# The end of a decoder block's kernel: last weight sums halved early, VectorE's order written down, last tile in two column halves

## The chip, the cores and the metric

One core of one Trainium2 chip runs the kernel. The metric is the device time of one execution in microseconds; the time of a kernel is the median of its runs. TensorE (PE) multiplies matrices into PSUM, VectorE (DVE) and ScalarE (ACT) work on rows of 128 partitions, GpSimd (POOL) takes some element-wise work early on, and SyncE (SP) issues the loads and stores. The engines run side by side and wait for each other through semaphores.

## What is computed

One layer of a hybrid decoder block: two attention branches over the same normed input, gated and merged. For 512 tokens of width 1024 it ends in these lines (u, the projections and both attentions stand ahead of them):

```python
y_mla = (o_mla * jax.nn.silu(z_mla)) @ w_br_mla[l]
...
y_fox = (o_fox * jax.nn.silu(z_fox)) @ w_br_fox[l]
mixed = (jax.nn.sigmoid(gate_a) * y_mla + jax.nn.sigmoid(gate_b) * y_fox) @ w_out[l]
h = h + rmsnorm(mixed, post_norm_g[l])
```

rmsnorm divides each token's row by the root of the mean of its squares, and multiplies by a gain per column. Only the last two lines concern the change.

## The kernel before

Nearly all the work is matmuls in a float32 form. Every operand x is split into hi, a rounded copy made by ScalarE, and lo = x - hi, made by VectorE; a product is three matmuls, hi x hi, hi x lo and lo x hi. A weight piece of 128 x 1024 thus costs a load or a sum, one conversion on ScalarE (`wh`, L130), and one subtraction on VectorE (`wl`, L103). `wh` and `wl` come from pools of three buffers each (`wp`), and a conversion waits until TensorE has left the buffer.

The product with `w_out` runs at the end. The contraction of 1024 is cut into two halves, the tokens into two halves of 256, the output columns into two halves of 512 (N0 and N1), and seven half-size products are formed in place of eight, from sums of weight blocks (`tb`, made earlier by VectorE from loaded blocks) and sums of token blocks (`mx`, halved into slices of `uT0`, called `s_[0]` to `s_[3]`, with hi and lo parts `sh` and `sl`). Each product has two pieces c of the contraction and two token tiles r of 128, and `block` (six matmuls of 128 x 512) does one (c, r). X[r], Z[r] and Y[r] are PSUM tiles of 128 x 512 float32. The order on TensorE, which is taken as written, is: X (plain weights, tokens `a1`), Y (plain, `a2`), Z (`summed(0)`, `s_[0]`), X (`summed(2)`, `s_[1]`), Z (plain, `s_[3]`), X (`summed(1)`, `s_[2]`, called w7), X (`summed(3)`, `a2`, called w4). X and Z keep adding onto what stands in them, and `yo` collects results of the four token tiles t = 0 to 3.

An output tile t ends so: ScalarE squares a half row and sums it (`squares_of`, L1120), VectorE scales that sum (`first_sum`, L1123), multiplies the row by the gain (`scaled_g`, L1127), ScalarE takes the root (L1130), VectorE the reciprocal (L1131), and for each column half VectorE multiplies by it and adds the input x (L1133), after which SP stores it (L1135). Tiles 0 and 1 finish during the product before the last and the last; tiles 2 and 3 need the last product, whose X[0] and X[1] hold their columns N0.

In the kernel before, w4's two pieces go through `summed`, as every sum does: conversion and subtraction into the pool's buffers shortly before the product. The second piece is queued behind VectorE's add that reads X[0] (L1165). The order on VectorE and ScalarE is that of a scheduler, which goes by priorities and by what it takes to be ready. The changed instructions are all behind 559 us.

Of the kernel before, what the change touches and what calls it, by code (L numbers as in the profile page):

```python
# [17 lines left out]
ALU = mybir.AluOpType  # L18
# [4 lines left out]
D = 1024  # L23
# [5 lines left out]
EPS = 1e-6  # L29
# [25 lines left out]
def block_kernel(ctx: ExitStack, tc: tile.TileContext, x, meta_tokens, pre_norm_g, w_in, fox_forget_b,  # L55
                 mla_q_norm_g, mla_kv_norm_g, w_uq, w_ukv, w_br_mla, w_br_fox, w_out, post_norm_g,
                 rope_tok, rope_pe, out):
    nc = tc.nc
# [43 lines left out]
    def split_lo(eng, lo, src, hi):  # L102
        return eng.tensor_tensor(out=lo, in0=src, in1=f32(hi), op=ALU.subtract)  # L103
# [159 lines left out]
    with ExitStack() as ph:  # L263
# [33 lines left out]
        for c in range(4):  # L297
            r = pa.tile([128, 2, NSM], F32, tag="wsr", name=f"wsr{c}", bufs=4)
# [145 lines left out]
        pin = tc.keep_in_program_order  # L444
# [74 lines left out]
        with tc.issue_after(lowered[("k", 1, 0), 1]):  # L519
            nc.vector.tensor_tensor_scan(out=fa[:, 0], data0=fa[:, 1], data1=fa[:, 2], initial=0.0, op0=ALU.add,  # L520
                                         op1=ALU.add)
        ch = pal.tile([NH, 2, L], F32R, tag="ch", name="ch")
        with tc.issue_after(halved[("k", 1, 0), 1]):
# [3 lines left out]
                                       op0=ALU.mult, op1=ALU.subtract)  # L527
# [21 lines left out]
    with ExitStack() as att:  # L549
# [451 lines left out]
    with ExitStack() as mg:  # L1001
# [89 lines left out]
        N0, N1 = slice(0, 512), slice(512, D)  # L1091
# [5 lines left out]
        def summed(n, c):  # L1097
            uid[0] += 1
            raw = tb[n][:, 2 * c : 2 * c + 2].rearrange("p k f -> p (k f)")
            return by_k(wsplit((uid[0], raw, [(0, 1024)], 1024))[0], 2)  # L1100

        def block(ps, a, t0, w, c, r, first, last, cs=slice(0, 512)):

            q = 0
            for kk in range(2):
                k = 2 * c + kk
                ts = slice(t0 + 128 * r, t0 + 128 * r + 128)
                for x, b in ((a[0], w[0]), (a[1], w[0]), (a[0], w[1])):
# [10 lines left out]
        def squares_of(src, t, n, w=512):  # L1119
            nc.scalar.activation(jk[:, :w], src, AF.Square, accum_out=ss[:, t, n : n + 1])  # L1120

        def first_sum(t, n):
            nc.vector.tensor_scalar(out=ss[:, t, 2:3], in0=ss[:, t, n : n + 1], scalar1=1.0 / D, scalar2=4.0 * EPS,  # L1123
                                    op0=ALU.mult, op1=ALU.add)

        def scaled_g(t, sl, src=None):
            nc.vector.tensor_tensor(out=yo[:, t, sl], in0=yo[:, t, sl] if src is None else src, in1=gp[:, sl], op=ALU.mult)  # L1127

        def finish_t(t, n, order):
            nc.scalar.activation(ss[:, t, 3:4], ss[:, t, n : n + 1], AF.Sqrt, bias=ss[:, t, 2:3], scale=1.0 / D)  # L1130
            nc.vector.reciprocal(ss[:, t, 3:4], ss[:, t, 3:4])  # L1131
            for sl_ in order:
                nc.vector.scalar_tensor_tensor(out=yo[:, t, sl_], in0=yo[:, t, sl_], scalar=ss[:, t, 3:4],  # L1133
                                               in1=xr[:, t, sl_], op0=ALU.mult, op1=ALU.add)
                nc.sync.dma_start(out2[128 * t : 128 * t + 128, sl_], yo[:, t, sl_])  # L1135

        X, Z = ([op5.tile([128, 512], F32, tag="po", name=f"{n}{r}") for r in range(2)] for n in "xz")
# [1 line left out]
        s_ = list(zip(sh, sl))  # L1139
# [15 lines left out]
        product(Z, s_[3], 0, lambda c: plain(1, 1, c), False, True)  # L1155
        w7 = [summed(1, c) for c in range(2)]
        for r in range(2):
            nc.vector.tensor_tensor(out=yo[:, r, N1], in0=Z[r], in1=yo[:, r, N1], op=ALU.add)
            squares_of(yo[:, r, N1], r, 1)
        w4 = [summed(3, 0)]  # L1160
        for c in range(2):
            for r in range(2):
                block(X, s_[2], 0, w7[c], c, r, False, False)
                if c:
                    read = nc.vector.tensor_tensor(out=yo[:, 2 + r, N1], in0=X[r], in1=yo[:, 2 + r, N1], op=ALU.add)  # L1165
# [59 lines left out]
```

## Time and profile before

| | us |
|---|---|
| median of 3 runs | 599.7 (599.19 to 601.25) |
| the profiled execution's own time | 599.22 |
| its span, first to last instruction | 597.2 |
| busy: TensorE, VectorE, ScalarE | 588.5, 383.0, 343.6 |
| last matmul ends | 591.16 |
| last store issued | 594.14 |

The profile is of one execution. A row gives the start in us from the span's start, the length in us, the engine, the line of the kernel, the operation, what it writes and reads, and how often it is repeated; in brackets stands how long the engine sat idle before it and what released it. Times of matmuls are modelled at their ends. In a group's row, "busy, mean ns" follows the bar.

### The profile page before, as it was taken

Reading aid. Unit: us, or ns where it says so; the run is one execution under the profiler, and the core shown is the slowest. Engines: PE = TensorE matmul, PEld = TensorE weight load, DVE = VectorE, ACT = ScalarE, POOL = GpSimd, SP = SyncE. Lnnn points to the kernel's source line nnn. Section 1 sums busy time; section 2 is a strip of 40 time slices with the busy share of each in tenths; the row PEclk is TensorE's granted clock in tenths of the full one; section 3 lists DMA queues with packets and bytes.
Section 4 is the critical chain, followed back from the end, with each engine's and each line's share of the span. In section 5 each row is a group of like instructions: output and inputs, shape, how many; then the busy total and the mean of one; then the engine's idle time right before and its main releaser. Section 6 shows DMA issues by size and latency. Waiting matters only on the chain.

```text
span 597.2 us, 10753 instructions
## 1 busy us (share of the span) xinstructions
PE 588.5 (99%) x3707; PEld 497.4 (83%) x3707; DVE 383.0 (64%) x1088; ACT 343.6 (58%) x786; POOL 201.0 (34%) x268
## 2 busy tenths in 40 slices
PE   8999999999999999999999999999999999999995
PEld 6889789889889888898898898878888888888884
DVE  6846776775775775757758747854634524367957
ACT  7847775784774775757748747842123423353753
POOL 4316746455458463554544544430000000000000
PEclk9999999999999999999999999999999999999999
DMA  8533799999986998896996887978523332333603
GB/s 293 117 80 98 152 173 252 211 201 230 170 198 117 222 223 215 183 192 161 173 203 164 195 162 154 193 168 295 168 78 99 105 106 72 105 106 104 213 2 140
DMA packets 219838, 96.91 MB, mean 162 GB/s; under 512 B 131552, under 2 KB 209768, under 8 KB 219784
## 3 DMA queue, kind: packets, MB, share of 16 engines
q1 hardware_dynamic: 219784, 96.23, 68.9%
q8 instruction: 29, 0.48, 0.3%
q14 instruction: 25, 0.20, 0.1%
HBM read 61.82 MB, written 3.97 MB: 110 GB/s over the span
## 4 chain that ended last, share of the span: by engine, by line
PE 95%; ACT 2%; DMA 1%; SPq 1%; issue 0%; DVE 0%; POOL 0%; DVEq 0%; ACTq 0%; POOLq 0%
PE z L97 17%; PE pg L97 15%; PE py L97 15%; PE v L97 9%; PE st L97 8%; PE fk L97 8%; PE fq L97 8%; PE ov L97 5%; PE x L97 4%; PE psm L97 2%; PE mq L97 2%; PE mk L97 1%; DMA wsr<-in_w_in_dram 1%; PE ppe L97 1%; PE y L97 1%; ACT uTh L373 0%
## 5 line engine op out<-in xcount | busy, mean ns | idle before, releaser
L103 POOL TENSOR_TENSOR wl<-wraw,wh 128x1024 fp32r<-128x1024 f32 (+2 forms) x62 | 119.7, 1937 | 95.3 <-ACT wh L130 72.3
L130 ACT CAST wh<-wraw 128x1024 fp32r<-128x1024 f32 (+1 forms) x80 | 83.2, 1042 | 115.6 <-PE pg L97 38.5
L799 ACT ACTIVATE sf<-sf,nb 128x272 f32<-128x272 f32 (+3 forms) x128 | 72.5, 567 | 16.7 <-DVE nb L791 15.4
L827 DVE SCALAR_TENSOR_TENSOR pn<-sf,ri,pn 128x128 f16<-128x128 f32 (+3 forms) x128 | 69.2, 579 | 6.9 <-ACT pn L826 6.6
L103 DVE TENSOR_TENSOR wl<-wraw,wh 128x1024 fp32r<-128x1024 f32 x34 | 41.6, 1223 | 42.4 <-ACT wh L130 42.4
L826 ACT ACTIVATE pn<-sf,ri 128x128 f16<-128x128 f32 (+3 forms) x128 | 61.3, 549 | 10.1 <-ACT sf L799 7.4
L97 PE MATMUL z<-uTh,wh 128*128 128x512 f32 x128 | 51.0, 398 | 0.0
L97 PE MATMUL pg<-uTh,wh 128*128 128x512 f32 x128 | 50.3, 393 | 0.0
L97 PE MATMUL z<-uTl,wh 128*128 128x512 f32 x128 | 50.1, 391 | 0.0
L97 PE MATMUL z<-uTh,wl 128*128 128x512 f32 x128 | 50.0, 391 | 0.0
L97 PE MATMUL pg<-uTl,wh 128*128 128x512 f32 x128 | 49.8, 389 | 0.0
L97 PE MATMUL pg<-uTh,wl 128*128 128x512 f32 x128 | 49.8, 389 | 0.0
L97 PE MATMUL py<-gh,wh 128*128 128x512 f32 x128 | 49.8, 389 | 0.0
L97 PE MATMUL py<-gl,wh 128*128 128x512 f32 x128 | 49.8, 389 | 0.0
L97 PE MATMUL py<-gh,wl 128*128 128x512 f32 x128 | 49.8, 389 | 0.0
L97 PE MATMUL st<-hlk,hlq 64*128 64x272 f32 (+3 forms) x480 | 46.0, 309 | 0.0
L97 PEld LDWEIGHTS st<-hlk,hlq 64*128 64x128 f32 x480 | 34.8, 185 | 6.0 <-ACT vh L714 2.8
L695 DVE TENSOR_REDUCE vsc<-v 128x1 f32<-128x272 f32 (+1 forms) x32 | 13.2, 432 | 37.8 <-PE v L97 37.8
L97 PE MATMUL v<-uTh,wl 128*128 128x256 f32 (+1 forms) x128 | 36.5, 285 | 0.0
L97 PE MATMUL fk<-uTl,wh 128*128 128x256 f32 (+1 forms) x128 | 36.4, 285 | 0.0
L97 PE MATMUL fk<-uTh,wh 128*128 128x256 f32 (+1 forms) x128 | 36.4, 285 | 0.0
L97 PE MATMUL v<-uTl,wh 128*128 128x256 f32 (+1 forms) x128 | 36.4, 285 | 0.0
(240 smaller groups left out, 1464.1 us busy)
## 6 DMA issues: line engine op xcount, KB each, us to landing
wraw<-in_w_in_dram SPq DMA_DIRECT2D x56, 512.0 KB, 4.5
wraw<-in_w_br_fox_dram SPq DMA_DIRECT2D x8, 512.0 KB
tb<-in_w_out_dram SPq DMA_DIRECT2D x8, 512.0 KB, 6.7
wraw<-in_w_br_mla_dram SPq DMA_DIRECT2D x8, 512.0 KB, 3.4
cbp<-c_dram SPq DMA_DIRECT2D x14, 264.0 KB, 5.4
wraw<-in_w_out_dram SPq DMA_DIRECT2D x6, 512.0 KB, 6.0
xr<-in_x_dram SPq DMA_DIRECT2D x4, 512.0 KB
out_dram<-yo SPq DMA_DIRECT2D x8, 256.0 KB, 2.0
```

What stands on the lines that cost most here:

```text
L97: nc.tensor.matmul(*a, **k)
L103: return eng.tensor_tensor(out=lo, in0=src, in1=f32(hi), op=ALU.subtract)
L130: nc.scalar.copy(wh[:, :n], raw[:, :n])
L695: nc.vector.tensor_reduce(out=sc[:, i : i + 1], in_=ps, op=ALU.max, axis=AX.X, apply_absolute_value=True)
L799: exps[g] = nc.scalar.activation(sf, sf, AF.Exp, bias=sums["nb"][:, h, b : b + 1], scale=-1.0, accum_out=sums["su"][:, h, b : b + 1]).ins
L826: nc.scalar.activation(hi, sf, AF.Copy, scale=rib)
L827: nc.vector.scalar_tensor_tensor(out=lo, in0=sf, scalar=rib, in1=hi, op0=ALU.mult, op1=ALU.subtract)
```

## The change

Three things change, all in the last part of the kernel. First, a new `put_in` makes hi and lo of the last weight sum `tb[3]` in buffers whose contents are no longer needed: piece 0 in `a1` (read last by the first X product), piece 1 in `s_[0]` (read last by the first Z product). Second, VectorE's instructions there are wrapped in `tc.keep_in_program_order` (`pin`), and the code is rewritten in the order that they are to have. Third, the last product goes tile by tile; for tile 3 the second piece of the contraction is done in two halves of 256 columns, each with its own square, sum and multiply, and the output columns N0 are finished and stored in the same two halves.

```diff
+        def put_in(n, c, to):
+            raw = tb[n][:, 2 * c : 2 * c + 2]
+            hi, lo = (t.rearrange("p k s -> p (k s)").rearrange("p (k f) -> p k f", k=2) for t in to)
+            nc.scalar.copy(hi, raw)
+            split_lo(nc.vector, lo, raw, hi)
+            return (lambda k: hi[:, k]), (lambda k: lo[:, k])
...
-        w4 = [summed(3, 0)]
+        w4 = [put_in(3, c, to) for c, to in enumerate((a1, s_[0]))]
+        for r in range(2):
+            scaled_g(r, N1)
+        finish_t(0, 1, (N0, N1))
         for c in range(2):
             for r in range(2):
                 block(X, s_[2], 0, w7[c], c, r, False, False)
-                if c:
-                    read = nc.vector.tensor_tensor(out=yo[:, 2 + r, N1], in0=X[r], in1=yo[:, 2 + r, N1], op=ALU.add)
-                    if not r:
-                        with tc.issue_after(read.ins):
-                            w4.append(summed(3, 1))
-                    squares_of(yo[:, 2 + r, N1], 2 + r, 1)
-                    first_sum(2 + r, 1)
         for r in range(2):
-            scaled_g(r, N1)
-            finish_t(r, 1, (N0, N1))
+            pin(nc.vector.tensor_tensor(out=yo[:, 2 + r, N1], in0=X[r], in1=yo[:, 2 + r, N1], op=ALU.add))
+            squares_of(yo[:, 2 + r, N1], 2 + r, 1)
+            if not r:
+                finish_t(1, 1, (N0, N1))
         for r in range(2):
+            first_sum(2 + r, 1)
             scaled_g(2 + r, N1)
-        for r in range(2):
-            for c in range(2):
-                block(X, a2, 256, w4[c], c, r, False, True)
-            squares_of(X[r], 2 + r, 0)
-            scaled_g(2 + r, N0, X[r])
-            finish_t(2 + r, 0, (N1, N0))
+        for c in range(2):
+            block(X, a2, 256, w4[c], c, 0, False, True)
+        squares_of(X[0], 2, 0)
+        scaled_g(2, N0, X[0])
+        finish_t(2, 0, (N1, N0))
+        block(X, a2, 256, w4[0], 0, 1, False, True)
+        cols = (slice(0, 256), slice(256, 512))
+        for i, sl in enumerate(cols):
+            block(X, a2, 256, w4[1], 1, 1, False, True, sl)
+            squares_of(X[1][:, sl], 3, (0, 3)[i], 256)
+            scaled_g(3, sl, X[1][:, sl])
+            if not i:
+                pin(nc.vector.scalar_tensor_tensor(out=ss[:, 3, 2:3], in0=ss[:, 3, 0:1], scalar=1.0 / D, in1=ss[:, 3, 2:3],
+                                                   op0=ALU.mult, op1=ALU.add))
+        finish_t(3, 3, (N1,) + cols)
```

The rest of the diff wraps VectorE's instructions in `first_sum`, `scaled_g` and `finish_t`, and Z's add, in `pin`. In the changed kernel's lines `scaled_g` is L1136, the reciprocal L1140, the final operation L1142, the adds of Z L1167 and of X L1177, and the small sum of tile 3 L1196.

The first place is VectorE from the adds of Z to the add of X[1] (x_6504), ahead of the last product; what an instruction waits for stands in brackets. Before:

```order
L1158 TENSOR_TENSOR yo<-z_6506,yo 128x512 [waits PE_49]
L103 TENSOR_TENSOR wl_6708<-tb_5497,wh_6707 128x1024 [waits Activation_49]
L1127 TENSOR_TENSOR yo<-yo,gp 128x512 [waits Activation_49]
L1131 RECIPROCAL pad<-pad 128x1 [waits Activation_49]
L1127 TENSOR_TENSOR yo<-yo,gp 128x512 [waits DVE_49]
L1133 SCALAR_TENSOR_TENSOR yo<-yo,pad,xr 128x512 [waits DMAHW5_49,DVE_49]
L1133 SCALAR_TENSOR_TENSOR yo<-yo,pad,xr 128x512
L1165 TENSOR_TENSOR yo<-x_6503,yo 128x512 [waits PE_49]
L103 TENSOR_TENSOR wl_6731<-tb_5497,wh_6730 128x1024 [waits Activation_49]
L1123 TENSOR_SCALAR pad<-pad 128x1 [waits Activation_49]
L1165 TENSOR_TENSOR yo<-x_6504,yo 128x512 [waits PE_49]
```

The same place in the changed kernel:

```order
L1167 TENSOR_TENSOR yo<-z_6506,yo 128x512 [waits PE_49]
L1136 TENSOR_TENSOR yo<-yo,gp 128x512 [waits Activation_49] x2
L1140 RECIPROCAL pad<-pad 128x1
L1142 SCALAR_TENSOR_TENSOR yo<-yo,pad,xr 128x512 [waits DMAHW5_49,DVE_49]
L1142 SCALAR_TENSOR_TENSOR yo<-yo,pad,xr 128x512
L1177 TENSOR_TENSOR yo<-x_6503,yo 128x512 [waits PE_49]
L1140 RECIPROCAL pad<-pad 128x1 [waits Activation_49]
L1142 SCALAR_TENSOR_TENSOR yo<-yo,pad,xr 128x512 [waits DMAHW6_49,DVE_49]
L1142 SCALAR_TENSOR_TENSOR yo<-yo,pad,xr 128x512
L1177 TENSOR_TENSOR yo<-x_6504,yo 128x512 [waits PE_49]
```

The two subtractions of w4 (wl_6708 and wl_6731) are gone from here, and tile 1's reciprocal and final operations have moved ahead of the add of X[1].

The second place is VectorE at the end, from the multiply of X[0] (tile 2) on. Before:

```order
L1127 TENSOR_TENSOR yo<-x_6503,gp 128x512 [waits Activation_49]
L1131 RECIPROCAL pad<-pad 128x1 [waits Activation_49]
L1133 SCALAR_TENSOR_TENSOR yo<-yo,pad,xr 128x512 [waits DMAHW7_49,DVE_49]
L1133 SCALAR_TENSOR_TENSOR yo<-yo,pad,xr 128x512
L1127 TENSOR_TENSOR yo<-x_6504,gp 128x512 [waits Activation_49]
```

In the changed kernel:

```order
L1136 TENSOR_TENSOR yo<-x_6503,gp 128x512 [waits Activation_49]
L1140 RECIPROCAL pad<-pad 128x1 [waits Activation_49]
L1142 SCALAR_TENSOR_TENSOR yo<-yo,pad,xr 128x512 [waits DMAHW7_49,DVE_49]
L1142 SCALAR_TENSOR_TENSOR yo<-yo,pad,xr 128x512
L1136 TENSOR_TENSOR yo<-x_6504,gp 128x256 [waits Activation_49]
L1196 SCALAR_TENSOR_TENSOR pad<-pad 128x1
L1136 TENSOR_TENSOR yo<-x_6504,gp 128x256 [waits Activation_49]
L1140 RECIPROCAL pad<-pad 128x1 [waits Activation_49]
```

The multiply of X[1] has become two of 256 columns, with the small sum between them, and the first of them stands behind tile 2's two final operations.

The third place is TensorE's last matmuls, those of tile 3 (x_6504). Before, the second piece is six matmuls of 512 columns, the last three of which repeat the three ahead of them:

```order
L97 MATMUL x_6504<-wh_6707,a2l 128x512
L97 MATMUL x_6504<-wl_6708,a2h 128x512
L97 MATMUL x_6504<-wh_6730,a2h 128x512
L97 MATMUL x_6504<-wh_6730,a2l 128x512
L97 MATMUL x_6504<-wl_6731,a2h 128x512
```

In the changed kernel, the end of the first half of the columns and the start of the second:

```order
L97 MATMUL x_6504<-uTh,a2h 128x256
L97 MATMUL x_6504<-uTh,a2l 128x256
L97 MATMUL x_6504<-uTl,a2h 128x256
L97 MATMUL x_6504<-uTh,a2h 128x256 [waits DVE_49]
L97 MATMUL x_6504<-uTh,a2l 128x256
```

The weights come from `uTh` and `uTl` (where `put_in` has put them), and the second half's first matmul waits for VectorE. The count that it waits for, 883, is the one to which the first half's multiply (L1136, 128x256) raises VectorE's semaphore.

More of the change, by code (lines that the diff above doesn't have):

```diff
@@ L1120, in squares_of @@
             nc.scalar.activation(jk[:, :w], src, AF.Square, accum_out=ss[:, t, n : n + 1])
+        pin = tc.keep_in_program_order
         def first_sum(t, n):
-            nc.vector.tensor_scalar(out=ss[:, t, 2:3], in0=ss[:, t, n : n + 1], scalar1=1.0 / D, scalar2=4.0 * EPS,
-                                    op0=ALU.mult, op1=ALU.add)
+            pin(nc.vector.tensor_scalar(out=ss[:, t, 2:3], in0=ss[:, t, n : n + 1], scalar1=1.0 / D, scalar2=4.0 * EPS,
+                                        op0=ALU.mult, op1=ALU.add))
         def scaled_g(t, sl, src=None):
-            nc.vector.tensor_tensor(out=yo[:, t, sl], in0=yo[:, t, sl] if src is None else src, in1=gp[:, sl], op=ALU.mult)
+            pin(nc.vector.tensor_tensor(out=yo[:, t, sl], in0=yo[:, t, sl] if src is None else src, in1=gp[:, sl], op=ALU.mult))
         def finish_t(t, n, order):
             nc.scalar.activation(ss[:, t, 3:4], ss[:, t, n : n + 1], AF.Sqrt, bias=ss[:, t, 2:3], scale=1.0 / D)
-            nc.vector.reciprocal(ss[:, t, 3:4], ss[:, t, 3:4])
+            pin(nc.vector.reciprocal(ss[:, t, 3:4], ss[:, t, 3:4]))
             for sl_ in order:
-                nc.vector.scalar_tensor_tensor(out=yo[:, t, sl_], in0=yo[:, t, sl_], scalar=ss[:, t, 3:4],
-                                               in1=xr[:, t, sl_], op0=ALU.mult, op1=ALU.add)
+                pin(nc.vector.scalar_tensor_tensor(out=yo[:, t, sl_], in0=yo[:, t, sl_], scalar=ss[:, t, 3:4],
+                                                   in1=xr[:, t, sl_], op0=ALU.mult, op1=ALU.add))
                 nc.sync.dma_start(out2[128 * t : 128 * t + 128, sl_], yo[:, t, sl_])
@@ L1157, in block_kernel @@
         for r in range(2):
-            nc.vector.tensor_tensor(out=yo[:, r, N1], in0=Z[r], in1=yo[:, r, N1], op=ALU.add)
+            pin(nc.vector.tensor_tensor(out=yo[:, r, N1], in0=Z[r], in1=yo[:, r, N1], op=ALU.add))
             squares_of(yo[:, r, N1], r, 1)
-        w4 = [summed(3, 0)]
+        w4 = [put_in(3, c, to) for c, to in enumerate((a1, s_[0]))]
+        for r in range(2):
+            scaled_g(r, N1)
+        finish_t(0, 1, (N0, N1))
         for c in range(2):
```

1 line of the change is left out of this document (added).

## The prediction

> **What bounds the kernel now.** I read the page's first part, then the chain of waits of the last 37 us, then the instructions of the last 15 us in order of time. Part 1 gives busy time, share and count.
>
> ```profile
> PE 588.5 (99%) x3707; PEld 497.4 (83%) x3707; DVE 383.0 (64%) x1088; ACT 343.6 (58%) x786; POOL 201.0 (34%) x268
> ```
>
> TensorE is busy 99% of 597.2 us, so only two things can move the time: a hole in TensorE's stream, and what follows its last matmul. The chain shows both (start, length, what; "issue" is time with no visible cause):
>
> ```profile
> 579.95 5.44 PE x L97 x24
> 585.38 0.01 issue
> 585.40 5.76 PE x L97 x24
> ...
> 591.68 0.20 ACT jk L1120
> ...
> 591.90 0.36 DVE yo L1127
> ...
> 592.51 0.17 DVE pad L1131
> ...
> 592.70 0.75 DVE yo L1133
> 593.45 0.66 DVEq L1221
> ```
>
> The last matmul ends at 591.16. Behind it come ScalarE's square (L1120), VectorE's multiply by the gain (L1127), reciprocal (L1131) and two final operations (L1133), then the last store. The last 24 matmuls take 5.76 us where the 24 before took 5.44. Instructions in order of time show why:
>
> ```profile
> 584.57 0.68 DVE L1165 TENSOR_TENSOR yo<-x,yo 128x512 f32<-128x512 f32 x1
> 585.00 0.39 PE L97 MATMUL x<-wl,uTh 128*128 128x512 f32 x1
> 585.40 0.47 PE L97 MATMUL x<-wh,a2h 128*128 128x512 f32 x1
> 585.71 0.39 PE L97 MATMUL x<-wh,a2l 128*128 128x512 f32 x1
> 585.94 0.39 PE L97 MATMUL x<-wl,a2h 128*128 128x512 f32 x1
> ```
>
> Matmuls start 0.23 apart (585.71 to 585.94). At 585.23 the last product should start to add onto X[0], but VectorE still reads X[0] until 585.25 (L1165). TensorE starts at 585.40, and the next start is 0.31 later: the hole costs 0.17 + 0.08 = **0.25 us**.
>
> **Part 1: weight sums halved early.** Of the last weight sum, both conversions and both subtractions (1.23 and 1.21 us on VectorE, at 580.84 and 585.17) go to places before and in the Z product. One conversion and one subtraction are moved into each of the two places. The rows that tell whether there is room:
>
> ```profile
> 561.82 1.23 DVE L103 TENSOR_TENSOR wl<-tb,wh 128x1024 fp32r<-128x1024 f32 x1 [0.62 <-ACT wh L130]
> 566.64 0.39 PE L97 MATMUL z<-wl,uTh 128*128 128x512 f32 x1
> 569.96 1.23 DVE L103 TENSOR_TENSOR wl<-wraw,wh 128x1024 fp32r<-128x1024 f32 x1 [1.50 <-ACT wh L130]
> ```
>
> At the first place VectorE waits for a conversion, then the new subtraction and the add of Y[0] go first: the old one ends at about 564.4 instead of 563.05. TensorE needs it at 566.64, so 2.2 us of cover are left. At the second place VectorE stands idle 1.50 us before each subtraction, as it does in every period of 2.7 us there, and the new one takes 1.23. ScalarE has the same holes (its conversion wh waits for TensorE to free a buffer). I cost it at **nothing**; if the cover went, each us would be a us of TensorE. SP's loads keep their order, and the halves need no new buffer.
>
> **Part 2: VectorE's written order.** Behind Z, without the two subtractions, VectorE's work goes as follows.
>
> ```profile
> 579.26 1.41 DVE L1158 TENSOR_TENSOR yo<-z,yo 128x512 f32<-128x512 f32 x2
> 580.71 0.59 ACT L1120 ACTIVATE jk<-yo 128x512 f32<-128x512 f32 x1
> 581.24 0.18 ACT L1120 ACTIVATION_READ_ACCUMULATOR jk<-yo 128x1 f32 x1
> 582.65 0.67 DVE L1127 TENSOR_TENSOR yo<-yo,gp 128x512 f32<-128x512 f32 x1
> ```
>
> The adds of Z end at 579.95 and 580.67 as before. A square with its readout takes 0.71, and the conversion that stood before the first one is gone: squares end at about 580.7 and 581.7, the multiplies at 581.4 and 582.4, tile 0's reciprocal and two final operations (0.15 and 1.41) at 583.9. X[0]'s sum is complete when the matmul of 583.64 ends (0.39), at 584.03; its add now finds VectorE free, ends near 584.75 and the hole at 585.40 closes: **-0.25 us** for all later matmuls. Tile 1's two final operations stand next, then the add of X[1], ending near 586.9; TensorE needs it at 588.23 - 0.25 = 587.98. Cover: about 1 us. Both tiles' stores also leave earlier, when the transfer engines are idle.
>
> **Part 3: tile 3 in two column halves.** Twelve half-width matmuls replace the last six. Rows of that width, before the halves' rows of the other engines:
>
> ```profile
> 46.76 0.28 PE L97 MATMUL fk<-uTh,wh 128*128 128x256 f32 x1
> 46.88 0.28 PE L97 MATMUL fk<-uTl,wh 128*128 128x256 f32 x1
> ```
>
> ```profile
> 18.31 0.39 ACT L409 ACTIVATE sm<-psm 128x256 f32<-128x256 f32 x1 [2.08 <-PE psm L97]
> 18.59 0.19 ACT L409 ACTIVATION_READ_ACCUMULATOR sm<-psm 128x1 f32 x1
> ```
>
> ```profile
> L717 DVE SCALAR_TENSOR_TENSOR vh<-v,vsc,vh 128x256 f16<-128x256 f32 x32 | 13.9, 475 | 0.0
> L103 DVE TENSOR_TENSOR hlk<-fk,hlk 128x256 fp32r<-128x256 f32 x8 | 3.4, 423 | 2.0 <-ACT hlk L250 2.0
> L1133 DVE SCALAR_TENSOR_TENSOR yo<-yo,pad,xr 128x512 f32<-128x512 f32 x8 | 5.7, 745 | 0.1
> ```
>
> Half-width matmuls start 0.12 apart, so twelve take 1.44 where six took 1.37. A half square with readout is 0.47 (18.31 to 18.78), a half multiply 0.42, a half final operation 0.475 (bounds 0.475 and 0.745, the nearer row taken).
>
> The order decides: the first matmul of the second half waits for VectorE, and the count that it waits for is raised by the multiply of the first half. TensorE may not add to columns 256 to 511 until ScalarE and VectorE have read columns 0 to 255. That multiply stands behind tile 2's two final operations on VectorE, so three steps fix the restart:
>
> ```profile
> 588.00 0.39 PE L97 MATMUL x<-wl,a2h 128*128 128x512 f32 x1
> 588.49 0.58 ACT L1120 ACTIVATE jk<-x 128x512 f32<-128x512 f32 x1 [0.63 <-PE x L97]
> 588.99 0.19 ACT L1120 ACTIVATION_READ_ACCUMULATOR jk<-x 128x1 f32 x1
> 589.61 0.68 DVE L1127 TENSOR_TENSOR yo<-x,gp 128x512 f32<-128x512 f32 x1
> 590.40 1.41 DVE L1133 SCALAR_TENSOR_TENSOR yo<-yo,pad,xr 128x512 f32<-128x512 f32 x2
> 590.75 0.40 PE L97 MATMUL x<-wl,a2h 128*128 128x512 f32 x1
> ```
>
> First, TensorE: r=1's first matmul at 587.98, six full ones (1.37), six halves, the last starting at 589.95 and ending at 590.24. ScalarE has squared the half by 590.75. Second, VectorE: tile 2's square starts 0.25 earlier (588.24) and is read out at 588.94; the multiply starts there, not at 589.61, 0.65 earlier, so the final pair ends at 591.81 - 0.65 = 591.16. Third, the half multiply ends at 591.5. From VectorE's end to the matmul was 0.15 at 585.40, so TensorE restarts at about 591.65, after 1.4 us of idling, and ends after 0.08 + 5 x 0.12 + 0.28 at **592.6**, 1.45 us later than now.
>
> From there: half square to 593.1; the half multiply and the root beside it to 593.5; reciprocal, and the first final operation at 593.7 (now 592.70, so +1.0; the halves give 0.45 back). Then 0.67 to the next start, 0.41, and 0.48: the last store is issued at 595.28, against
>
> ```profile
> 594.14 0.33 SPq L1135 DMA_DIRECT2D out_dram<-yo  x1
> ```
>
> that is +1.14. The transfers themselves, by stretches (stretch, length, PE, PEld, DVE, ACT, POOL, clock, DMA share, GB/s):
>
> ```profile
> 594.00:594.40 0.40, 0.00 (x0) 0.00 (x0) 0.11 (x1) 0.00 (x0) 0.00 (x0) 1.00 0.15 61
> 594.40:594.80 0.40, 0.00 (x0) 0.00 (x0) 0.00 (x0) 0.00 (x0) 0.00 (x0) 1.00 1.06 415
> ...
> 595.60:596.00 0.40, 0.00 (x0) 0.00 (x0) 0.00 (x0) 0.00 (x0) 0.00 (x0) 1.00 0.17 56
> ```
>
> Two stores of 256 KB pass at about 400 GB/s from 594.35 to 595.65, 0.65 each, the first some 0.85 behind its issue (593.48). Now the last one is 128 KB in pieces half as long. Bounds: 0.33 at the same rate, 0.65 if a piece costs the same whatever its length. At 0.33 the data ends at 596.6 (+1.0), at 0.43 at 596.8 (+1.2), at 0.65 at 597.3 (+1.65). I take the near end, **+1.1 us** in all.
>
> **A rule against the change.** In the rows above VectorE's multiply of X[1] starts at 591.90, right behind ScalarE's readout (591.68 + 0.20), though VectorE was free at 591.81 and the matmuls had ended; X[1], 512 columns of float32, is read by one engine at a time. The Trainium skill, "PSUM — Partial Sum Buffer", section "Summary: rules for kernel authors", tells authors who read PSUM while a matmul runs to use a different bank and to guard with semaphores by bank. By that rule both halves of X[1] are one bank and the split buys no overlap (+1.1); were columns the unit, it would give -0.5. The trace agrees for the two readers; it has no row of a matmul beside a reader of the same tile.
>
> **Rivals.** (A) *The halves overlap as meant*: TensorE runs on and ends at 590.96, ScalarE takes the second half at 591.46, VectorE (pair until 591.16, two half multiplies, the small sum between them, root, reciprocal) starts the final operations at 592.1 instead of 592.70, and the last data ends 0.4 to 0.6 earlier: -0.5 us. Against it: the wait stands in the program. (B) *The change doesn't do what it says at its front*: the hole at 585.40 stays, since its waiter still waits for the same add, and only the serial end is added: +1.35. It would need VectorE's add to end 0.35 us behind my working (584.75; it must be out by 585.08). (C) *VectorE's written order becomes TensorE's bound*: tile 1's final pair stands ahead of X[1]'s add. If VectorE is more than 1 us later there than worked out, TensorE stops at 587.98, and each further us is paid in full. A VectorE late by 2 us, about one more pair (1.41) and a multiply (0.67), gives +1.1 + 1.0 = +2.1 us, past 0.3%. Against it: every duration in that order is a row of this trace, and two subtractions have gone.
>
> **How the numbers follow.** The profiled execution took 599.22 (span 597.2, 2.0 around it); with the three runs (599.19, 599.7, 601.25) the middle of the four is 599.46. The sum gives 600.3 on the profiled execution's footing and about 600.6 for a usual run, +0.18%. A measurement here tells about 0.3% (1.8 us) from no change. Chances: my forecast 0.68, A 0.10, B 0.10, C 0.12. The forecast's own upper end (long pieces 0.5 more, slower halves 0.2 more: +1.8) puts 0.14 of it, and the upper end of B 0.03, past 1.8 us. With C that makes slower 0.29; A beside a lucky pair of runs leaves 0.05 for faster; 0.66 is within 0.3%. Range: from A (599.0) to the upper bounds together (601.7).
>
> **What would show it.** Right: no gap ahead of the last product; a gap of 1.2 to 1.6 us in TensorE between its last two groups of six half-width matmuls, ended by VectorE's half multiply (L1136); the last matmul 1.3 to 1.6 later than 591.15; about 1.05 from there to the first L1142 instead of 1.55. Wrong: half-width matmuls without a gap (A), a gap still at the product's start (B), a gap ahead of r=1's first matmul (C), or matmuls at a lower granted clock after the gap; the clock stays 1.00 until 596 in the last stretch quoted, 4.8 us behind the last matmul.

## The result, and the profile after

The changed kernel takes 600.53 us, the median of 22 runs (600.03 to 601.69), beside 599.75 us for the kernel before in 22 runs of the same series (598.63 to 601.27). The ratio is 1.0016, with a 95% interval of 1.0010 to 1.0022: slower by about a sixth of one per cent. That is within the 0.3% that the prediction took as the least that can be told from no change, but 22 runs of each are enough to tell it. The median lies 0.07 us from the forecast. The profiled execution took 600.4 us, with a span of 598.5.

The first part of the changed kernel's page gives busy time, share and count of each engine:

```profile
PE 588.1 (98%) x3713; PEld 498.3 (83%) x3713; DVE 383.4 (64%) x1091; ACT 343.6 (57%) x788; POOL 201.1 (34%) x268
```

The busy times have hardly moved, although the span is 1.3 us longer: what is new is waiting. The chain of work that ended last, of the last stretch, shows where (start, length, what):

```profile
580.23 8.22 PE x L97 x36
590.05 1.41 DVE yo L1142 x2
591.46 0.35 DVE yo L1136
...
591.85 0.98 PE x L97 x6
...
593.90 0.75 DVE yo L1142
```

Before, the chain stayed with TensorE up to its last matmul. Now the chain leaves TensorE for VectorE at 590.05, goes through tile 2's two final operations and the first half's multiply, and comes back to TensorE for only six matmuls. The rows in order of time show each place of the prediction:

```profile
552.76 0.39 PE L97 MATMUL x<-wh,a1h 128*128 128x512 f32 x1
...
563.39 1.22 DVE L103 TENSOR_TENSOR wl<-tb,wh 128x1024 fp32r<-128x1024 f32 x1
...
571.68 1.23 DVE L103 TENSOR_TENSOR uTl<-tb,uTh 128x1024 fp32r<-128x1024 f32 x1 [0.20 <-ACT uTh L1105]
...
584.35 0.69 DVE L1177 TENSOR_TENSOR yo<-x,yo 128x512 f32<-128x512 f32 x1 [0.17 <-PE x L97]
585.28 0.39 PE L97 MATMUL x<-wl,uTh 128*128 128x512 f32 x1
585.51 0.39 PE L97 MATMUL x<-a1h,a2h 128*128 128x512 f32 x1
586.48 0.68 DVE L1177 TENSOR_TENSOR yo<-x,yo 128x512 f32<-128x512 f32 x1
588.27 0.40 PE L97 MATMUL x<-a1h,a2h 128*128 128x512 f32 x1
590.25 0.28 PE L97 MATMUL x<-uTl,a2h 128*128 128x256 f32 x1
...
590.85 0.19 ACT L1127 ACTIVATION_READ_ACCUMULATOR jk<-x 128x1 f32 x1
591.38 0.42 DVE L1136 TENSOR_TENSOR yo<-x,gp 128x256 f32<-128x256 f32 x1
591.85 0.38 PE L97 MATMUL x<-uTh,a2h 128*128 128x256 f32 x1 [1.32 <-DVE yo L1136]
592.55 0.28 PE L97 MATMUL x<-uTl,a2h 128*128 128x256 f32 x1
593.90 1.54 DVE L1142 SCALAR_TENSOR_TENSOR yo<-yo,pad,xr 128x512 f32<-128x512 f32 x3
595.58 0.41 SPq L1144 DMA_DIRECT2D out_dram<-yo  x1
```

The last product now starts without a hole (585.28 to 585.51, 0.23), since VectorE's add of X[0] is done at 585.04. Between the two column halves of tile 3 TensorE stands still: 590.25 to 591.85 is 1.60 from start to start where 0.12 is usual, and the bracket names VectorE's multiply of the first half. The last matmul ends at 592.83.

One correction is needed before these times are set against the old ones. The first matmul of the `w_out` products starts at 552.76 here. In the trace of before:

```profile
552.48 0.39 PE L97 MATMUL x<-wh,a1h 128*128 128x512 f32 x1
```

TensorE's instructions ahead of that matmul are the same in both kernels, and the change begins behind it, so 0.28 us of the span's difference is put down to the execution and not to the change. (Over all ten traces of this document that matmul starts between 552.33 and 554.05.) From here on the **end part** is compared: the span less the start of that matmul. It was 44.72 us before (597.2 - 552.48) and is 45.74 after (598.5 - 552.76): +1.02 us. Spans are printed to 0.1 us, and each kernel has one profiled execution, so differences of end parts below 0.1 us mean nothing.

### The profile page after: what moved, and what is told of

It is laid out like the page before. It is cut to its first block, busy times and chain, and to the rows that moved or that the text cites. A ratio compares the mean times of both kernels' runs of the same rounds, so it can differ in the third digit from the quotient of the medians.

```text
span 598.5 us, 10770 instructions
## 1 busy us (share of the span) xinstructions
PE 588.1 (98%) x3713; PEld 498.3 (83%) x3713; DVE 383.4 (64%) x1091; ACT 343.6 (57%) x788; POOL 201.1 (34%) x268
## 4 chain that ended last, share of the span: by engine, by line
PE 92%; ACT 2%; DMA 2%; DVE 2%; issue 1%; POOL 1%; SPq 0%; DVEq 0%; ACTq 0%; POOLq 0%
PE z L97 15%; PE py L97 15%; PE pg L97 14%; PE v L97 9%; PE fk L97 8%; PE st L97 8%; PE fq L97 8%; PE ov L97 5%; PE x L97 3%; PE psm L97 3%; PE mq L97 2%; PE mk L97 1%; DMA pt<-pn 1%; PE ppe L97 1%; PE y L97 1%
## 5 line engine op out<-in xcount | busy, mean ns | idle before, releaser
L103 POOL TENSOR_TENSOR wl<-wraw,wh 128x1024 fp32r<-128x1024 f32 (+2 forms) x62 | 119.7, 1938 | 96.0 <-ACT wh L130 72.3
L103 DVE TENSOR_TENSOR wl<-wraw,wh 128x1024 fp32r<-128x1024 f32 x34 | 41.6, 1223 | 41.7 <-ACT wh L130 41.6
```

## The experiments

The theory: the early sums and the written order save 0.25 us, and the halves of tile 3 cost about 1.35 us, because both halves lie in one PSUM tile, so that the second half's matmuls wait until the first half has been read. Its rivals: the cost lies in the narrower operations or the additional store, or in VectorE's order. "End part" is worked out as above from each kernel's trace.

| kernel | first matmul | span | end part | against before | median us | ratio to before, 95% |
|---|---|---|---|---|---|---|
| before | 552.48 | 597.2 | 44.72 | | 599.82, 599.35 in the two series | |
| after | 552.76 | 598.5 | 45.74 | +1.02 | 600.53 | 1.0016 (1.0010 to 1.0022) |
| e1_whole_tile3 | 553.64 | 598.1 | 44.46 | -0.26 | 599.38 | 0.9992 (0.9983 to 1.0001) |
| e2_halves_alone | 553.17 | 599.6 | 46.43 | +1.71 | 601.28 | 1.0029 (1.0017 to 1.0040) |
| e3_two_banks | 552.33 | 597.2 | 44.87 | +0.15 | 599.87 | 0.9997 (0.9986 to 1.0008) |
| e4_multiply_first | 554.05 | 599.5 | 45.45 | +0.73 | 600.97 | 1.0021 (1.0012 to 1.0030) |
| e5_put_in_alone | 552.92 | 597.5 | 44.58 | -0.14 | 599.41 | 0.9998 (0.9990 to 1.0007) |
| e6_order_alone | 553.30 | 602.5 | 49.20 | +4.48 | 603.57 | 1.0067 (1.0051 to 1.0083) |
| e7_pool_quarter | 554.01 | 599.6 | 45.59 | +0.87 | 600.59 | 1.0017 (1.0009 to 1.0026) |
| e8_reads_last | 553.73 | 598.9 | 45.17 | +0.45 | 600.22 | 1.0014 (1.0006 to 1.0023) |

e1 to e4 ran in one series and e5 to e8 in another; each ratio is against the runs of before in its own series. The changed kernel ran in a third, against 599.75.

### e1: tile 3 whole again

The changed kernel with tile 3 done as before the change:

```diff
-        block(X, a2, 256, w4[0], 0, 1, False, True)
-        cols = (slice(0, 256), slice(256, 512))
-        for i, sl in enumerate(cols):
-            block(X, a2, 256, w4[1], 1, 1, False, True, sl)
...
-        finish_t(3, 3, (N1,) + cols)
+        for c in range(2):
+            block(X, a2, 256, w4[c], c, 1, False, True)
+        squares_of(X[1], 3, 0)
+        scaled_g(3, N0, X[1])
+        finish_t(3, 0, (N1, N0))
```

> The changed kernel with tile 3 whole again (six matmuls of 512 columns, one square, one multiply, two final operations and stores); the early halved sums and the written order stay. My theory (the front of the change closes a 0.25 us hole, the column halves cost the rest through the wait of the second half for the first half's multiply): no gap in TensorE anywhere in the last product, 0.25 us faster than the kernel before (ratio 0.9996), 1.2 us faster than the changed kernel. Rival (the loss comes from the written order or the early sums, which crowd VectorE and ScalarE): still about 1 us slower than before (1.0016).

The end part is 0.26 us shorter than before, and 1.28 shorter than after. The rows of TensorE at the start of the last product and at its end, and VectorE's last pair:

```profile
586.16 0.39 PE L97 MATMUL x<-wl,uTh 128*128 128x512 f32 x1
586.39 0.39 PE L97 MATMUL x<-a1h,a2h 128*128 128x512 f32 x1
...
591.70 0.40 PE L97 MATMUL x<-uTl,a2h 128*128 128x512 f32 x1
...
593.65 1.42 DVE L1142 SCALAR_TENSOR_TENSOR yo<-yo,pad,xr 128x512 f32<-128x512 f32 x2
```

No hole (0.23), no gap: 24 matmuls from 586.39 to 591.70 are 0.23 apart on average. So the first two parts of the change save about a quarter of a microsecond, and the halves turn that into a loss. The whole-run ratio, 0.9992, is not clear of no change; the end part tells it.

### e2: the halves alone

The kernel before, with only its last product written as in the change, and the small sum unpinned:

```diff
-        for r in range(2):
-            for c in range(2):
-                block(X, a2, 256, w4[c], c, r, False, True)
-            squares_of(X[r], 2 + r, 0)
-            scaled_g(2 + r, N0, X[r])
-            finish_t(2 + r, 0, (N1, N0))
...
+        for i, sl in enumerate(cols):
+            block(X, a2, 256, w4[1], 1, 1, False, True, sl)
+            squares_of(X[1][:, sl], 3, (0, 3)[i], 256)
+            scaled_g(3, sl, X[1][:, sl])
...
+        finish_t(3, 3, (N1,) + cols)
```

> The kernel before with only the column halves of tile 3. My theory: the hole at the start of the last product stays, tile 2's final pair ends at 591.8 as before, so the first half's multiply ends at 592.15, TensorE idles about 1.8 us between the halves, the last matmul ends near 593.3, and the whole is 1.65 us slower than before (1.0028). Rival (the halves are harmless, the loss lies in the front): within 0.3 us of before.

+1.71 us, as expected. VectorE's pair of tile 2, its half multiply, and the matmul that waits:

```profile
591.10 1.42 DVE L1133 SCALAR_TENSOR_TENSOR yo<-yo,pad,xr 128x512 f32<-128x512 f32 x2
...
592.43 0.42 DVE L1127 TENSOR_TENSOR yo<-x,gp 128x256 f32<-128x256 f32 x1
...
592.91 0.38 PE L97 MATMUL x<-wh,a2h 128*128 128x256 f32 x1 [1.76 <-DVE yo L1127]
```

Here TensorE idles 1.76 us, longer than the 1.32 of the changed kernel. VectorE still carries the late subtractions, reaches tile 2's pair later, and the half multiply stands behind that pair. So the two parts of the change at its front also shorten the wait that its third part makes: the halves cost 1.71 without them and 1.02 + 0.26 = 1.28 with them.

### e3: the second half in a PSUM tile of its own

The changed kernel, with columns 256 to 511 of X[1] in another accumulator from the first X product on. The matmuls, copies and adds of X[1] are therefore all issued in two pieces of 256 columns:

```diff
+        X1 = [X[1][:, 0:256], acc("x1b")[:, 0:256]]
...
-            squares_of(X[1][:, sl], 3, (0, 3)[i], 256)
-            scaled_g(3, sl, X[1][:, sl])
+            squares_of(X1[i], 3, (0, 3)[i], 256)
+            scaled_g(3, sl, X1[i])
```

> The changed kernel with X[1] split by columns into two PSUM tiles (the right half in a third buffer of the accumulators' pool) from the first product on, so that all matmuls of r=1 in the X products are of 256 columns (84 more halves in place of 42 whole ones: +0.47 us of TensorE). My theory (what stops the second half is that both halves are one PSUM tile): no gap between the halves; the last matmul ends 0.2 us later than before, the last store's data 0.15 earlier: 0.9998 against before, 1.1 us faster than the changed kernel. Rival (VectorE's queue, not the shared tile, decides the end): no more than 0.3 us faster than the changed kernel.

The gap is gone. The last matmul of the first half, the first of the second (`x1b`), and the readers:

```profile
590.34 0.28 PE L97 MATMUL x<-uTl,a2h 128*128 128x256 f32 x1
590.46 0.28 PE L97 MATMUL x1b<-uTh,a2h 128*128 128x256 f32 x1
...
591.42 0.37 ACT L1133 ACTIVATE jk<-x1b 128x256 f32<-128x256 f32 x1 [0.29 <-PE x1b L97]
591.42 0.42 DVE L1142 TENSOR_TENSOR yo<-x,gp 128x256 f32<-128x256 f32 x1
```

The matmuls are 0.12 apart across the boundary. ScalarE reads the second half while VectorE reads the first, both from 591.42, where in the changed kernel every reader of X[1] follows the other. This settles the cause of the gap: the same halves, operations and stores, in two tiles, lose nothing there.

It gained less than expected, though, +0.15 against -0.15. Two things in the trace account for it. The last matmul ends 38.99 us behind the start of the first (591.04 + 0.28 - 552.33), where e1's does so 38.46 behind (591.70 + 0.40 - 553.64): 48 matmuls of X[1] in the four X products have become pairs of 256 columns, a pair takes 0.238 us (95 starts of halves in 11.29 us) and a whole one 0.229, which makes 0.4 of these 0.5 us. And the end is not shortened by the halved store, which a look over all kernels shows below.

### e4: the first half's multiply ahead of tile 2's final pair

```diff
-        finish_t(2, 0, (N1, N0))
+        root_t(2, 0)
...
                 pin(nc.vector.scalar_tensor_tensor(out=ss[:, 3, 2:3], in0=ss[:, 3, 0:1], scalar=1.0 / D, in1=ss[:, 3, 2:3],
                                                    op0=ALU.mult, op1=ALU.add))
+                finish_t(2, None, (N1, N0))
```

`root_t` is the root and the reciprocal out of `finish_t`; the pair follows behind the first half's multiply.

> The changed kernel with the first half's multiply (and the small sum behind it) ahead of tile 2's two final operations in VectorE's order. My theory: in the changed kernel's trace the multiply starts 0.34 us after ScalarE's readout, held by VectorE's queue; here it starts right behind the readout, TensorE's gap shrinks by 0.3, tile 2's pair runs beside the second half, and the whole is 0.3 us faster than the changed kernel (1.0011 against before). Rival (the queue on VectorE is all of the loss): 1 us faster than the changed kernel. Rival (it is none of it): no difference.

```profile
591.54 0.28 PE L97 MATMUL x<-uTl,a2h 128*128 128x256 f32 x1
...
592.13 0.19 ACT L1127 ACTIVATION_READ_ACCUMULATOR jk<-x 128x1 f32 x1
592.36 0.42 DVE L1136 TENSOR_TENSOR yo<-x,gp 128x256 f32<-128x256 f32 x1 [1.06 <-ACT jk L1127]
...
592.84 0.38 PE L97 MATMUL x<-uTh,a2h 128*128 128x256 f32 x1 [1.02 <-DVE yo L1136]
```

The multiply now starts right behind ScalarE's readout (592.13 + 0.19, then 592.36), where in the changed kernel it stood 0.34 longer in VectorE's queue (readout done at 591.04, start at 591.38). The gap shrinks from 1.60 to 1.30, and the end part by 0.29. What is left of the gap is the reading itself: matmul's end, half square, readout, half multiply, one after the other. The whole-run ratio, 1.0021, does not show the gain; the expected 1.0011 lies just outside its interval. The end part's +0.73 us would be 1.0012, at the interval's lower edge; where the rest comes from stays open.

### e5: the early sums alone

The kernel before with `put_in`, no written order and no halves:

```diff
-        w4 = [summed(3, 0)]
+        w4 = [put_in(3, c, to) for c, to in enumerate((a1, s_[0]))]
...
-                    if not r:
-                        with tc.issue_after(read.ins):
-                            w4.append(summed(3, 1))
```

> The kernel before with only the early halved sums (no written order, tile 3 whole). My theory: the two subtractions between Z and the last product were what kept VectorE from X[0]'s add; the scheduler's order without them puts that add behind tile 1's first final operation, so it ends at about 585.1 and the hole shrinks from 0.25 us to about 0.1: 0.15 to 0.25 us faster than before (0.9997); from the first matmul that writes x to the span's end 44.5 us (44.72 before, 45.74 in the changed kernel). Rival (the written order is what closes the hole): no change, 44.7.

```profile
584.78 0.68 DVE L1172 TENSOR_TENSOR yo<-x,yo 128x512 f32<-128x512 f32 x1
585.45 0.39 PE L97 MATMUL x<-wl,uTh 128*128 128x512 f32 x1
585.68 0.40 PE L97 MATMUL x<-a1h,a2h 128*128 128x512 f32 x1
```

The hole is closed (0.23; about 0.1 of it was expected to stay), without any written order: the early sums are the part that closes it. Little was to spare. The add ends at 585.46, and before the change 0.15 us lay between the end of this add and the matmul that waited for it (585.25 to 585.40), so the matmul could have started at 585.61 and started at 585.68. In the changed kernel, with the written order, the same reckoning leaves 0.32 us (585.51 - 585.04 - 0.15). Beyond this margin e5 and e1 show no gain from the order: the last matmul ends 38.48 us behind the start of the first in e5 (591.00 + 0.40 - 552.92) and 38.46 in e1, and 38.67 in before (590.75 + 0.40 - 552.48).

### e6: the written order alone

e1, with the sums made late through the pool as before:

```diff
-        w4 = [put_in(3, c, to) for c, to in enumerate((a1, s_[0]))]
+        w4 = [summed(3, c) for c in range(2)]
```

> The kernel before with only the written order (tile 3 whole, the last sums through the pool's buffers; the second subtraction, which waits for TensorE to leave a buffer, then stands ahead of tile 0's multiply in VectorE's order). My theory: the order needs the early sums; VectorE stands until ScalarE's last conversion at about 584, X[0]'s add ends near 588.5, TensorE stops some 3.3 us ahead of the last product: 3.2 us slower than before (1.0054), 47.9 us from the first matmul that writes x to the end. Rival (the order alone gives the gain): 0.25 us faster, 44.5.

Slower by 4.48 us in the end part, 1.3 more than expected. The rows of VectorE and TensorE around the start of the last product:

```profile
584.39 1.22 DVE L103 TENSOR_TENSOR wl<-tb,wh 128x1024 fp32r<-128x1024 f32 x1 [1.50 <-ACT wh L130]
585.83 0.39 PE L97 MATMUL x<-wl,uTh 128*128 128x512 f32 x1
588.26 0.68 DVE L1177 TENSOR_TENSOR yo<-x,yo 128x512 f32<-128x512 f32 x1
589.09 0.47 PE L97 MATMUL x<-wh,a2h 128*128 128x512 f32 x1 [2.87 <-DVE pad L1140]
590.28 0.63 PE L97 MATMUL x<-wh,a2l 128*128 128x512 f32 x1
```

The second subtraction waits 1.50 us for its conversion, and in a written order everything behind it waits too: the multiplies of tiles 0 and 1, tile 0's final pair, then the add of X[0], which ends only at 588.94. TensorE stands 3.26 from start to start; that much was expected. The rest is a lower clock in this execution, in the stretches of the same kernel (length, PE, PEld, DVE, ACT, POOL, clock, DMA share, GB/s):

```profile
585.80:589.00 3.20, 0.41 (x2) 0.00 (x0) 3.17 (x7) 0.03 (x1) 0.00 (x0) 1.00 0.14 55
...
589.80:593.20 3.40, 3.40 (x9) 2.65 (x9) 2.67 (x6) 0.72 (x2) 0.00 (x0) 0.51 0.43 164
```

For 3.4 us the granted clock is 0.51 (then 0.99 again), and eight matmuls, from 589.87 to 593.26, start 0.42 apart instead of 0.23: 8 x 0.2 = 1.6 us. With 3.26 - 0.23 for the wait and 0.08 for the late start behind it (589.09 to 589.40) that makes 4.7, which is what e6 loses to e1 (49.20 - 44.46 = 4.74). How far the clock fell in the other executions, 602.02 to 605.44 us long, is not known. So the two parts at the front depend on each other in one direction: this written order needs the early sums, the sums do not need the order. An order that puts the second late sum behind the add of X[0], as the kernel before has it, was not tried.

### e7: a quarter of the last final operation on ScalarE and GpSimd

e1 with columns 768 to 1023 of N1 scaled on ScalarE and added on GpSimd, beside VectorE:

```diff
-        finish_t(3, 0, (N1, N0))
+        finish_t(3, 0, (slice(512, 768), slice(768, D), N0))
...
+                if sl_ == slice(768, D):
+                    nc.scalar.activation(yo[:, t, sl_], yo[:, t, sl_], AF.Copy, scale=ss[:, t, 3:4])
+                    nc.gpsimd.tensor_tensor(out=yo[:, t, sl_], in0=yo[:, t, sl_], in1=xr[:, t, sl_], op=ALU.add)
```

> The kernel with the early sums and the written order and tile 3 whole, and a quarter of tile 3's last work moved: columns 768 to 1023 are scaled by ScalarE and added by GpSimd while VectorE does the other three quarters. My theory (behind the last reciprocal the end is set by VectorE's two operations and, just as closely, by 512 KB of stores at 400 GB/s that begin 0.85 us behind the first issue): the first store leaves 0.27 us earlier, so 0.2 us faster than with tile 3 whole and all on VectorE (44.25 us from the first matmul that writes x to the end, against 44.46; 0.9992 against before). Rival (GpSimd's start or its sharing with VectorE costs more): 44.5 or more.

The forecast fell: the end part grew by 1.13 over e1. ScalarE's and GpSimd's quarter, and SP's last three stores:

```profile
594.01 0.51 ACT L1143 ACTIVATE yo<-yo,pad 128x256 f32<-128x256 f32 x1 [0.50 <-DVE pad L1140]
594.65 1.09 POOL L1144 TENSOR_TENSOR yo<-yo,xr 128x256 f32<-128x256 f32 x1 [200.07 <-ACT yo L1143]
594.52 2.05 SPq L1148 DMA_DIRECT2D out_dram<-yo  x3
```

The add took 1.09 us for 256 columns and ends at 595.74. Sixteen subtractions of the same shape that GpSimd makes earlier in this kernel (L103) take 0.74 on average; why this add is slower is not shown, so it stays open which of the rival's two reasons holds. SP issues in order, so the store of N0, ready at 595.16 when VectorE's two operations (594.01 + 1.15) are done, stands behind the store that waits for GpSimd.

### e8: both halves' matmuls ahead of all reads

The changed kernel, with the second half's matmuls issued ahead of the first half's square and multiply:

```diff
         for i, sl in enumerate(cols):
-            block(X, a2, 256, w4[1], 1, 1, False, True, sl)
+            if not i:
+                for s in cols:
+                    block(X, a2, 256, w4[1], 1, 1, False, True, s)
```

> The changed kernel with both column halves' matmuls ahead of both halves' squares and multiplies, so that nothing is read from X[1] until TensorE is done. My theory (the wait between the halves is the loss; the half widths themselves cost little): no gap, the last matmul ends 0.3 us earlier than before, but ScalarE and VectorE take turns on the one PSUM tile, four half steps in a row (about 0.45 us longer than the two whole ones), and three final operations take 0.15 longer: 0.3 us slower than before (1.0005), 0.7 us faster than the changed kernel, 45.0 us from the first matmul that writes x to the end. Rival (the half-width steps are the loss, not the wait): 45.7 as in the changed kernel.

```profile
591.92 0.28 PE L97 MATMUL x<-uTl,a2h 128*128 128x256 f32 x1
592.24 0.37 ACT L1127 ACTIVATE jk<-x 128x256 f32<-128x256 f32 x1 [1.73 <-PE x L97]
592.74 0.42 DVE L1136 TENSOR_TENSOR yo<-x,gp 128x256 f32<-128x256 f32 x1 [0.32 <-ACT jk L1127]
593.20 0.37 ACT L1127 ACTIVATE jk<-x 128x256 f32<-128x256 f32 x1 [0.49 <-DVE yo L1136]
...
594.24 1.54 DVE L1142 SCALAR_TENSOR_TENSOR yo<-yo,pad,xr 128x512 f32<-128x512 f32 x3
```

TensorE has no gap, with one tile and the same halves: so the gap needs a read between the halves' matmuls, not narrow matmuls. But the two readers now take turns four times (square, multiply, square, multiply, each behind the other), and 591.92 + 0.28 to 594.24 is 2.04 us where the changed kernel needs 1.07 and e1 1.55. The kernel ends 0.57 sooner than after and 0.71 later than e1. The whole-run ratio, 1.0014, has 1.0006 as its lower end, just above the expectation; the end part's +0.45 us would be 1.0008, inside the interval.

## Why the prediction was right

Its sum was +1.1 us and the end part measured +1.02; its time was 600.6 us and the median 600.53. That the time fits to 0.07 us is in part luck: the prediction started from 599.46 for the kernel before, which took 599.75 in the longer series, and the medians differ by 0.78 us and not by 1.1. The steps are the better test. Since the profiled execution came to the `w_out` products 0.28 us later, its times are given less 0.28.

| step of the prediction | predicted | measured |
|---|---|---|
| old weight sum at the first place ends | 564.4 | 563.39 + 1.22 - 0.28 = 564.33 |
| hole ahead of the last product | none | none (585.28, 585.51) |
| cover of X[1]'s add | about 1 | 588.27 - (586.48 + 0.68) = 1.11 |
| tile 2's pair ends | 591.16 | 591.46 - 0.28 = 591.18 |
| TensorE restarts | 591.65 | 591.85 - 0.28 = 591.57 |
| last matmul ends | 592.6 | 592.83 - 0.28 = 592.55 |
| from there to the first L1142 | about 1.05 | 593.90 - 592.83 = 1.07 |
| last store issued | 595.28 | 595.58 - 0.28 = 595.30 |

**The gap.** The prediction took the wait from the program: the second half's first matmul waits for the count that the first half's multiply raises. e3 and e8 show that this is the cause: the gap goes when the halves lie in two tiles, and when nothing is read between them. The three steps that fixed the restart (TensorE, VectorE's pair, the half multiply) held to within 0.1 us; of the 0.08 us by which TensorE restarted early, most is the step from the multiply's end to the matmul, 0.05 us (591.38 + 0.42 to 591.85) where the prediction put the 0.15 of the add at 585.40. And e4 measures the one place in VectorE's queue that they spoke of, 0.3 us.

**The hole.** Its removal was put at -0.25. e1's end part gives -0.26 and its last matmul -0.21 (38.46 against 38.67), and e5 shows that the early sums do it. The early work itself was put at nothing, and that held: from 552.76 to 590.25 no two matmuls of the changed kernel start more than 0.24 us apart, the second new subtraction (571.68) included.

**The end.** Here the prediction said two things that are not the same. It gave the last store's issue, +1.14, and bounds for the end of the data, 596.6 to 597.3 (+1.0 to +1.65). The bounds do not follow from the last store's issue. They come out if the data begin at about 595.3, some 0.85 us behind the first store's issue, and tile 3's pieces then pass without a break (595.3 + 0.65 + 2 x 0.33 = 596.6). The traces bear out this second way. From the first final operation of tile 3 (its L1142 or the like) to the end of the span they show (e7, which does this work otherwise, is left out):

| | kernels | us |
|---|---|---|
| N0 finished and stored whole | before, e1, e5, e6 | 4.50, 4.45, 4.54, 4.52 |
| N0 finished and stored in halves | after, e2, e3, e4, e8 | 4.60, 4.67, 4.67, 4.62, 4.66 |

Halving costs 0.1 to 0.2 us there and saves nothing. Stretches of the changed kernel's end show why it saves nothing (last two columns DMA share and GB/s):

```profile
595.20:595.60 0.40, 0.00 (x0) 0.00 (x0) 0.24 (x1) 0.00 (x0) 0.00 (x0) 1.00 0.20 82
595.60:596.00 0.40, 0.00 (x0) 0.00 (x0) 0.00 (x0) 0.00 (x0) 0.00 (x0) 0.88 1.01 389
...
596.80:597.20 0.40, 0.00 (x0) 0.00 (x0) 0.00 (x0) 0.00 (x0) 0.00 (x0) 0.50 0.25 80
```

Transfers begin at about 595.5 and end at about 596.88 without a break: tile 3's 512 KB pass at some 380 GB/s from the moment that the first of its stores gets through, whatever the sizes of the others. So in these kernels the end is set by the first final operation and the bytes, and not by the last store's issue. The first final operation starts 0.92 later than before (593.90 - 0.28 - 592.70; predicted +1.0), and the data end 0.95 later (596.88 - 0.28 - 595.65); the prediction's range for the data, +1.0 to +1.65, began just above. From the first final operation to the end of the data the changed kernel thus takes 2.98 us and the kernel before 2.95, so most of the 0.1 to 0.2 us that halving costs lies behind the last data; what takes it there is not shown. Between 596.40 and 596.80, when by these rates only pieces of half the length were left, 374 GB/s passed, which is near the rate of the whole pieces (389 just before): of the prediction's two bounds the near one holds.

**The rule against the change.** The prediction set beside its readers' row what the Trainium skill says in "PSUM — Partial Sum Buffer", section "Summary: rules for kernel authors": who reads PSUM while a matmul runs is to use a different bank. The runs agree with it in what it cost here: in one tile TensorE waited 1.32 us in the changed kernel and 1.76 us in e2, or the readers took turns behind it (e8); in two tiles (e3) there was no gap. Whether this chip could run a matmul beside a reader of the same tile wasn't tried; the kernels here wait, and their time is that of waiting.

**The rivals.** A (overlap) would have had no gap; it needs e3's second tile, and even then e3 stays at +0.15, not -0.5: with its narrower matmuls the last one ends 0.32 us later than before (38.99 against 38.67), so the first final operation comes only 0.02 earlier (592.53 - 552.33 against 592.70 - 552.48), and the end behind it takes 0.17 longer. B (the hole stays) is seen in no kernel with the early sums; in e2, without them, it stayed (starts at 585.69 and 586.10). C (VectorE late at X[1]'s add) had 1.11 us of cover. Its mechanism is real at another place: in e6 a written order with one late instruction holds TensorE for 3 us. The clock, named among what would make the prediction wrong, stayed at 1.00 in the gap of the changed kernel:

```profile
590.50:591.80 1.30, 0.03 (x1) 0.00 (x0) 1.30 (x4) 0.47 (x2) 0.00 (x0) 1.00 0.09 36
```

The prediction's ground for this, that the clock held for 4.8 us behind the last matmul of the kernel before, was weak: in e1 it fell some 2.3 us behind (last section).

**What stays open.** End parts come from one execution each, and the differences of the medians do not follow them closely: against before, the medians of e4, e7 and e8 lie about 0.4 us higher than their end parts say (e4: 600.97 - 599.82 = 1.15, against 0.73), those of e2, e6 and the changed kernel about 0.25 lower. Whether that is the choice of the profiled execution or an effect of the program ahead of the `w_out` products was not settled. The best version is e1, early sums and written order with tile 3 whole: 0.26 us off the end part, and a ratio of 0.9992 that is not clear of no change.

## What to carry to other kernels

Halving a result's columns so that its readers start earlier gave no overlap here while both halves lay in one PSUM tile; in two tiles the wait went, but the kernel was still slower at its end than with the tile whole (+0.15 against -0.26). In one tile, find the wait of the second half's first matmul and count the reader's queue up to the instruction that it names, since TensorE paid all of it. Taking an operation off the engine that reads an accumulator can close a hole in TensorE's stream though that engine is far from busy, and a written order for that engine is safe only if nothing in it is late. At the end of a kernel, ask what bounds the last transfers: when it is their bytes, only an earlier first store helps, and a smaller last one does not.

## What the runs showed of the hardware

In e6, a TensorE idle of 2.87 us was followed, some 0.8 us after the matmuls had started again, by 3.4 us at a granted clock of 0.51, while gaps of 1.32 us (after) and 1.76 us (e2) were followed by no slower matmuls. Behind the last matmul the clock falls at quite different distances, as worked out from the granted clock of stretches of 0.4 us: some 2.3 us behind in e1 (0.96 in 594.00 to 594.40; the last matmul ends at 592.10), 3.1 us in the changed kernel (0.88 in 595.60 to 596.00) and 5.2 us in before (0.95 in 596.00 to 596.40). So the length of the idling alone does not decide when the clock falls. The Trainium skill, "TensorE: Matmul & The Clock Gate", Part 1, says that the clock halves after an idle window of about 3.4 us, and that these windows run freely. The length of the slow stretch agrees with that figure, and the spread of the distances fits windows that run freely; the idles that came ahead of the falls in e6 and e1 were shorter than one window.

A GpSimd add of 128 x 256 float32 took 1.09 us in e7, beside 0.74 for the mean of sixteen subtractions of that shape in the same kernel. Stores in pieces of half the length moved at 374 GB/s, beside 415 in the best stretch shown of before.
